# Routed experts on one core: weights in rows of 16 KB, tokens gathered by slot, two experts combined at once

## The chip, the core and the metric

The kernel runs on one core of a Trainium2 chip. A core has TensorE (PE, with its weight loads shown apart as PEld), VectorE (DVE), ScalarE (ACT), GpSimd (POOL) and SyncE (SP, which here only issues transfers), and 16 DMA engines that bring data from the chip's memory (HBM) into the on-chip memory of 128 partitions. The metric is the time of one launch in microseconds (us) on the device. The profiler records one launch with every instruction and every DMA packet; its span is the time from the first instruction to the last.

## The reference, cut to what matters

The program is two blocks of a model on 256 tokens of 1024 features in float32. The first block has two attentions, then the part that this change is about, then a gated embedding; the second block is a gated convolution and pooling, twice. The part in question sends every token to 4 of 32 experts:

```python
def routed_experts(h, w_router, b_router, w_gate_up, b_gate_up, w_down, b_down):
    logits = (hf @ w_router).astype(jnp.float32) + b_router.astype(jnp.float32)
    top_vals, top_idx = lax.top_k(logits, TOP_K)
    top_w = jax.nn.softmax(top_vals, axis=-1)
...
    def expert_block(args):
        xb, e = args
        gu = xb @ w_gate_up[e] + b_gate_up[e]
        g, u = gu[:, :D_EXPERT], gu[:, D_EXPERT:]
        g = jnp.minimum(g, SWIGLU_LIMIT)
        u = jnp.clip(u, -SWIGLU_LIMIT, SWIGLU_LIMIT)
        glu = g * jax.nn.sigmoid(SWIGLU_ALPHA * g)
        return ((u + 1.0) * glu) @ w_down[e] + b_down[e]
...
    y = jax.ops.segment_sum(yr * row_w[:, None].astype(yr.dtype), row_tok, num_segments=n + 1)[:n]
```

The sum y is added to the residual X. The weights of one expert are w_gate_up[e], 1024 x 2048 floats (8.39 MB), and w_down[e], 1024 x 1024 floats (4.19 MB): 12.58 MB for an expert and 402.7 MB for the 32. Each byte is used once.

## The kernel before, in words

Everything up to the router runs first. It leaves X (the residual), XS (the normed tokens, without their gains), and for each expert and token a rank in RM (its place among the tokens of that expert) and a weight in W. Then all 32 experts are computed one after the other by `static_expert`, each with 64 slots for tokens; what an expert has beyond 64 tokens is left to `further_block`, which runs in a loop behind a branch and isn't entered with these inputs.

For one expert, `load` issues on SP's queue 8 transfers of gate_up and 4 of down, each of 1 MB into a tile of 2048 columns. Row k * 128 + p of gate_up lies in partition p of tile k, so a partition gets one row of 8 KB; of down a tile holds two such rows of 4 KB. The tiles come from the pool `ring2`, 17 of them. A transfer is issued as soon as its tile is free and its turn on SP's queue has come. The products of the weights are 96 matmuls of 512 columns (64 for gate and up, 32 for down), each two instructions in the profile; they are those from `raw` to `bank`.

Around them, for each expert: `gather` makes a matrix of ones and zeros, OH, from the ranks (L777) and multiplies XS by it in 16 matmuls, of which XG, the tokens of the expert with features on partitions, comes out (L779 to L782, recorded at L150 as those of OH and XS); OW (L784) is the same with the weights in it, turned in two transposes (L810) and copied (L812). The activations of gate and up are on DVE and ACT (L803 to L807); their result is transposed (L823), copied (L825) and multiplied by down; the product is copied to yr (L832). `combine` then multiplies yr by the turned OW, 4 matmuls with the weights on 64 partitions, and adds each to X (L838 to L840).

Two things aren't in the order in which they are written. `combine` of expert e and `gather` for e + 1 are put behind the last product of gate and up (`gu_end`, with `issue_after`), so that they lie between those products and the ones of down. A scheduler of the language orders the rest by what is ready. The matmul helper `mm` is line L150, the transfers of `load` L176, those of `load_split` L193 with its scaled copies L198, and `row_rstd` has its squares at L284.

Behind the last expert, `ring2` is closed, and a new pool p3 takes the same memory: eight tiles for the rows of w_ple_gate are loaded into it, scaled on ACT (L198, `se`, `Yh` and `hi`), and their low halves made on POOL (L985, L987) or DVE (L989). Then the branch to the further blocks follows; behind it X is transposed (L946) and squared (L284), and the rest of the program runs.

Of the kernel before, what the change touches and what calls it, by code (L numbers as in the profile page):

```python
# [22 lines left out]
SL = 64  # L23
# [6 lines left out]
# columns of the constants that depend on shapes alone  # L30
# [12 lines left out]
# rows that every partition gets  # L43
# [52 lines left out]
def block_kernel(ctx: ExitStack, tc: tile.TileContext, a, out, dbg=None, ne=NE):  # L96
# [19 lines left out]
    def pair(at=None):  # L116
        """Room for the halves of 1024 columns."""
# [34 lines left out]
    def mm3(o, l, r, start, stop):  # L152
        """float32 product of operands split in halves of 12 bits each."""
# [4 lines left out]
    def split(raw, dst, eng=None):  # L158
        """raw = dst[0] + dst[1], both exact in the tensor engine's short float32."""
# [7 lines left out]
    def load(src, cn, size=2048, at=None):  # L167
        """Rows of src over (k, partition), a tile at a time, in turn in the tiles at where they are given."""
# [42 lines left out]
    tiles = {"adr": [ada_slot() for _ in range(3)]}  # L211
    hh, hl = [slot(s, dt=FR).rearrange("p (k n) -> p k n", k=KD) for s in ("s0", "s1")]
# [4 lines left out]
    wu, vv = slot("s2", 2560), slot("s5")  # L217
# [146 lines left out]
    # the rotated part of the keys that the heads share  # L364
# [6 lines left out]
    def rope(dst, src, T, half_, eng=None):  # L371
        """dst = src * cos + swapped src * sin, for heads [128, heads, 2 * half_] with the table of a token tile."""
# [7 lines left out]
    def head_root(src, hd, extra=None):  # L380
        """(mean of squares + eps) ** -0.5 of the heads [128, heads, d] over hd features."""
# [9 lines left out]
    roots_a, marks = [], []  # what fills gaps is issued behind the marks  # L391
# [32 lines left out]
    # the norm along the tokens, on every partition  # L424
# [61 lines left out]
    def values(hp, prs, Vt, dst):  # L486
        """The values of two heads, feature-major, in halves."""
# [104 lines left out]
    def branch_weights(n):  # L592
        """A tile for each 256 columns."""
# [5 lines left out]
    # sigmoid(z) = (tanh(z / 2) + 1) / 2; the half follows the output projection  # L599
# [23 lines left out]
    # the biases of gate and up: row p has expert p % 32's, low halves where p // 32 is odd,  # L623
    # the columns h * 512 to h * 512 + 511 of both for h = p // 64
# [31 lines left out]
    def logits(XT, h, pl):  # L656
        """The transposed half of X[:, t] times the router's weights; the norm's factor follows."""
# [72 lines left out]
    def further_list():  # L730
        """The further blocks of 64 rows of the experts that got more than 64."""
# [16 lines left out]
        # a row of the list for each partition that has one: its place, then its expert and first rank  # L748
# [471 lines left out]
```

## Time and profile before

| what | value |
|---|---|
| three runs | 1451.78, 1452.36, 1454.26 us; median 1452.36 |
| the profiled execution | span 1451.8 us, as long as the fastest run |
| PE busy | 1385.2 us (95%) |
| DVE, ACT, POOL busy | 594.2, 319.3, 320.9 us |
| bytes moved | 502.56 MB, mean 346 GB/s |
| time from the first expert's L803 to the last one's | 248.99 to 1172.49 us |
| granted TensorE clock, mean | 0.983 |

The page of a profile gives busy times over the whole span, then the span in 40 slices of 36.3 us. Slices 6 to 31 are the experts. A busy share there says that an engine had instructions running, not that it set the pace: PE and the DMA engines are both near full in these slices, and which of them the other waits for is seen only in the waits and in the timeline.

### The profile page before, as it was taken

The page shows a single profiled execution, that of the slowest core. Times are in us where ns is not written, and L with a number is a line of the kernel's source. Part 1 is how long each engine was busy: PE and PEld are TensorE (multiplying, and loading weights), DVE is VectorE, ACT ScalarE, POOL GpSimd, SP SyncE. Part 2 cuts the span into 40 slices and gives each one's busy share as a digit, 9 for nine tenths or more (in the row PEclk, how much of TensorE's full clock was granted, in tenths as well). Part 3 has the DMA queues.
Part 4 walks back from the last instruction along what each step waited for, and adds up shares of the span by engine and source line. Part 5 has one row for each costly group of instructions (what it writes and reads, how often), then busy time and mean ns, then how long its engine had stood idle before and what let it go on. Part 6 is the DMA issues. An engine that isn't in the chain of part 4 may idle for free. (4 is left out here: it accounts for less than half of the span.)

```text
span 1451.8 us, 18980 instructions
## 1 busy us (share of the span) xinstructions
PE 1385.2 (95%) x7599; PEld 795.1 (55%) x7599; DVE 594.2 (41%) x973; ACT 319.3 (22%) x598; POOL 320.9 (22%) x353
## 2 busy tenths in 40 slices
PE   7989999999999999999999999999999998889987
PEld 6788886344444444444443344444444347887986
DVE  4898954121322132213222222221321138688685
ACT  6745531000000000000000000000001135435432
POOL 5595461000000000000000000000000035785682
PEclk9989998999999999999999999999999999999999
DMA  9738789999999999999999999999999955756651
GB/s 332 239 119 305 263 305 401 417 417 418 417 415 416 418 418 416 415 417 418 418 416 416 417 417 418 417 415 417 417 418 415 417 226 189 232 176 202 202 190 44
DMA packets 144586, 502.56 MB, mean 346 GB/s; under 512 B 10288, under 2 KB 63792, under 8 KB 111472
## 3 DMA queue, kind: packets, MB, share of 16 engines
q1 hardware_dynamic: 143936, 500.60, 88.0%
q8 instruction: 61, 1.00, 0.3%
q10 hardware_dynamic: 560, 0.72, 0.2%
q14 instruction: 29, 0.24, 0.0%
HBM read 500.24 MB, written 1.05 MB: 345 GB/s over the span
## 5 line engine op out<-in xcount | busy, mean ns | idle before, releaser
L150 PE MATMUL bank<-raw,mid 128*64 128x512 f32 x3072 | 680.3, 598 | 1.9 <-ACT mid L825 1.4
L150 PEld LDWEIGHTS bank<-raw,mid 128*64 128x64 f32 x3072 | 215.1, 138 | 414.9 <-issue 387.9
L803 DVE TENSOR_SCALAR mid<-bank 128x512 f32<-128x512 f32 x32 | 22.1, 691 | 443.7 <-PE bank L150 443.7
L855 POOL CAST BIAS<-BIAS 128x128 fp32r<-128x128 f32 x32 | 10.2, 321 | 852.5 <-PE bank L150 852.4
L165 DVE TENSOR_TENSOR lo<-raw,hi 128x1024 fp32r<-128x1024 f32 (+2 forms) x91 | 116.1, 1296 | 21.3 <-ACT hi L160 20.9
L150 PE MATMUL bulk<-OH,XS 128*128 128x64 f32 x1024 | 121.6, 278 | 1.6 <-DVE OH L777 1.6
L150 PEld LDWEIGHTS bulk<-OH,XS 128*128 128x128 f32 x1024 | 120.2, 196 | 2.6 <-DVE OH L777 1.8
L160 ACT CAST hi<-raw 128x1024 fp32r<-128x1024 f32 (+1 forms) x102 | 105.8, 1041 | 68.0 <-PE bulk L150 57.5
L805 ACT ACTIVATE mid<-mid 128x512 f32<-128x512 f32 x32 | 20.1, 629 | 390.6 <-DVE mid L803 390.6
L150 PE MATMUL bulk<-mid,small 64*128 64x512 f32 x256 | 99.2, 628 | 7.1 <-DVE X L840 6.4
L784 DVE TENSOR_SCALAR OW<-cst,RM,SW 128x128 f32<-128x128 f32 x64 | 19.3, 344 | 172.1 <-PE bank L810 172.1
L840 DVE TENSOR_TENSOR X<-X,bulk 128x512 f32<-128x512 f32 x128 | 81.7, 679 | 9.0 <-PE bulk L150 9.0
L165 POOL TENSOR_TENSOR lo<-raw,hi 128x512 fp32r<-128x512 f32 x50 | 72.9, 1484 | 40.1 <-ACT hi L160 35.3
L812 ACT COPY small<-bank 128x256 f32<-128x256 f32 x32 | 11.9, 372 | 290.2 <-PE bank L810 290.2
L150 PEld LDWEIGHTS bulk<-mid,small 64*128 64x128 f32 x256 | 31.0, 185 | 74.8 <-issue 40.4
L150 PE MATMUL bulk<-hi,s 128*128 128x256 f32 (+2 forms) x256 | 59.3, 323 | 7.9 <-ACT hi L160 7.4
L150 PE MATMUL bulk<-s,hi 128*128 128x256 f32 x320 | 63.7, 296 | 0.0
L782 DVE TENSOR_TENSOR mid<-bulk,VC 128x512 f32<-128x512 f32 x32 | 22.1, 691 | 90.9 <-PE bulk L150 90.9
L556 DVE SCALAR_TENSOR_TENSOR acc<-adr,cact,acc 128x512 f32<-128x512 f32 x49 | 55.5, 1133 | 0.8 <-DMA adr<-in_w_ada_dram 0.3
L150 PEld LDWEIGHTS bulk<-s,hi 128*128 128x128 f32 x320 | 51.8, 197 | 1.0 <-DVE s L609 0.4
L559 POOL TENSOR_TENSOR adr<-adr,cact 128x512 f32<-128x512 f32 x32 | 44.5, 1412 | 34.3 <-DMA adr<-in_w_ada_dram 34.3
L150 PEld LDWEIGHTS bulk<-hi,s 128*128 128x128 f32 x256 | 43.9, 195 | 11.6 <-ACT hi L160 7.4
(442 smaller groups left out, 1906.0 us busy)
## 6 DMA issues: line engine op xcount, KB each, us to landing
raw<-in_w_gate_up_dram SPq DMA_DIRECT2D x256, 1024.0 KB, 19.8
raw<-in_w_down_dram SPq DMA_DIRECT2D x128, 1024.0 KB, 20.0
raw<-in_w_in_dram SPq DMA_DIRECT2D x75, 512.0 KB, 5.1
adr<-in_w_ada_dram SPq DMA_DIRECT2D x48, 512.0 KB, 4.5
raw<-in_w_out_dram SPq DMA_DIRECT2D x23, 512.0 KB, 3.8
raw<-in_w_ple_gate_dram SPq DMA_DIRECT2D x5, 512.0 KB, 15.8
raw<-in_w_branch_b_dram SPq DMA_DIRECT2D x4, 512.0 KB, 7.3
raw<-in_w_branch_a_dram SPq DMA_DIRECT2D x4, 512.0 KB, 5.4
```

What stands on the lines that cost most here:

```text
L150: nc.tensor.matmul(o, l, r, start=start, stop=stop)
L160: nc.scalar.copy(dst[0], raw)
L165: (eng or nc.vector).tensor_sub(dst[1][..., cs], raw[..., cs], dst[0][..., cs].bitcast(F32))
L556: e.scalar_tensor_tensor(v, w[:, k], cact[:, i + k:i + k + 1], v, op0=OP.mult, op1=OP.add)
L559: e.tensor_mul(w[:, k:k + 2], w[:, k:k + 2], cact[:, i + k:i + k + 2].unsqueeze(2).to_broadcast([P, 2, n]))
L782: nc.vector.tensor_mul(XG, pX.rearrange("p (k n) -> p k n", k=KD), bcol("g_ffn", 0, KD, SL))
L784: nc.vector.tensor_scalar(OW[:, t], io64d, rank(t), wgt(t), op0=OP.is_equal, op1=OP.mult)
L803: nc.vector.tensor_scalar(g_, pG, 7.0, None, op0=OP.min)
L805: nc.scalar.activation(sg, g_, AF.Sigmoid, scale=1.702)
L812: nc.scalar.copy(OT, pT[:, :S])
L840: nc.vector.tensor_add(xv, xv, pc)
L855: nc.gpsimd.tensor_copy(bs, ONE[:, e, :, None].bitcast(F32).to_broadcast([P, 2, SL]))
```

## The change

There are three parts. **Loads**: a new function, `load_rows`, puts r rows that follow one another in memory into one partition: 2 rows of gate_up (2 x 8 KB) or 4 rows of down (4 x 4 KB), so 16 KB without a gap. A tile has 4096 columns (2 MB), an expert 6 of them, and ring2 has 8 tiles, with OW and a new tile Y beside them. The order of the features in the products follows (XG's columns, `u[:, c::4]`, and new gains `g_rows`). **Gather**: OH becomes the operand that is held and XS the one that streams, so 4 matmuls of 512 columns give the tokens with slots on partitions; ACT copies them (XT), 4 transposes turn them, and DVE multiplies by the gains. **Combine**: OW of two experts lies in one tile, turned by 4 transposes for every second expert (`turn`), and split into a matrix of ones (OT) and the weights by slot (ws); the product of down is scaled by ws and kept in Y as a high half (ACT) and a low half (DVE) in the short float32 type; two experts are added to X by 8 matmuls over all 128 partitions.

```diff
-            return phase["ring2"].tile([P, 2048], F32, name="raw2", tag="raw2")
+            return phase["ring2"].tile([P, 4096], F32, name="raw2", tag="raw2")
...
+    def load_rows(src, cn, r, at=None):
+        blocks = src.rearrange("(b p r) n -> b p r n", p=P, r=r)
+        nb, parts = src.shape[0] // (P * r), {}
+        pr = r if at is None else 2048 // cn
+        def piece(b, i):
+            if (b, i) not in parts:
+                raw = (raw_slot() if at is None else at[len(parts) % len(at)])[:, :pr * cn]
+                raw = raw.rearrange("p (r n) -> p r n", r=pr)
+                nc.sync.dma_start(raw, blocks[b, :, i * pr:(i + 1) * pr])
...
-    def gather(rank, wgt):
+    def gather(rank, wgt, q, ow):
...
-            for k in range(KD):
-                mm(pX[:, k * SL:(k + 1) * SL], XS[:, t, k * P:(k + 1) * P], OH[:, t], t == 0 and k == 0,
-                   t == NT - 1 and k == KD - 1)
-        XG = mid([P, KD, SL])
-        nc.vector.tensor_mul(XG, pX.rearrange("p (k n) -> p k n", k=KD), bcol("g_ffn", 0, KD, SL))
...
+        for t in range(NT):
+            for g in range(2):
+                mm(pX[g * SL:(g + 1) * SL], OH[:, t], XS[:, t, g * 512:(g + 1) * 512], t == 0, t == NT - 1)
+        XT = mid([P, 512])
+        nc.scalar.copy(XT, pX)
+        pt = bulk()
+        for c in range(4):
+            nc.tensor.transpose(pt[:, c * P:(c + 1) * P], XT[:, (c // 2) * 256 + c % 2:(c // 2 + 1) * 256:2], ident)
+        XG = mid([P, 4, 2, SL])
+        nc.vector.tensor_mul(XG.rearrange("p c g n -> p (c g) n"), pt.rearrange("p (k n) -> p k n", k=KD),
+                             bcol("g_rows", 0, KD, SL))
...
+    def turn(ow):
+        pT = bank()
+        for i in range(2):
+            for t in range(NT):
+                nc.tensor.transpose(pT[:, (i * NT + t) * P:(i * NT + t + 1) * P],
+                                    ow[:, t, 2 * i:2 * i + 2].rearrange("p c n -> p (c n)"), ident)
+        OT, ws = mid([P, 2, S], FR), tiny([P, 2], "ws")
+        p3_ = pT.rearrange("p (i n) -> p i n", i=2)
+        nc.vector.tensor_scalar(OT, p3_, 0.0, None, op0=OP.is_gt)
+        nc.vector.reduce_sum(ws, p3_, axis=AX)
...
-        gu = load(gu_src, 2 * DE, at=at)
-        dn = load(dn_src, D) if at is None else None
+        gu = load_rows(gu_src, 2 * DE, 2, at)
+        dn = load_rows(dn_src, D, 4) if at is None else None
...
-        yr = mid([P, 512])
-        nc.scalar.copy(yr, py)
...
+        for g in range(2):
+            h, sl = g ^ q, slice(g * SL, (g + 1) * SL)
+            nc.scalar.activation(Y[sl, 0, h], py[sl], AF.Copy, scale=ws[sl, h:h + 1])
+            nc.vector.scalar_tensor_tensor(Y[sl, 1, h], py[sl], ws[sl, h:h + 1], Y[sl, 0, h].bitcast(F32),
+                                           op0=OP.mult, op1=OP.subtract)
...
+                for i in range(2):
+                    mm(pc, OT[sl, h, t * P:(t + 1) * P], Y[sl, i, h], i == 0, i == 1)
...
-    ready = gather(*rank_of(0))
-    ring2 = tc.tile_pool(name="ring2", bufs=17, reuse_waits="tile")
+    ring2 = tc.tile_pool(name="ring2", bufs=8, reuse_waits="tile")
+    pair_["ow"] = ow_tile()
+    ready = gather(*rank_of(0), 0, pair_["ow"])
```

The line numbers grow by 22 to 78: `mm` is L152 after the change, the transfers of `load_rows` are L197, `load_split` is L215 with its copies at L220, `turn` has L828, the transposes of XT L814, those of the activations L867, the high half of Y L878 and `row_rstd` L306.

On PE, the first place is around the end of the products of gate and up of one expert in the middle of the loop (`raw_...` are the tiles of weights, `mid` the yr, XG and activations, `small` the turned OW). Before, between the last gate_up tile and the first product of down there are combine, the transposes of the activations and the gather; the turned OW comes behind the biases:

```order
L150 MATMUL bank<-raw_4068,mid 64x512 x4
L150 MATMUL bulk<-mid,small 128x512 x4
L823 MATMUL bank<-cst,mid 128x128 x4
L150 MATMUL bulk<-OH,XS 128x64 x16
L150 MATMUL bank<-raw_4070,mid 64x512 x4
L150 MATMUL bank<-raw_4072,mid 64x512 x4
```

After the change two kinds of boundary take turns, here one without and one with a combine (both in the order in which PE has them):

```order
L152 MATMUL bank<-raw_3986,mid 64x512 x8
L152 MATMUL bulk<-XS,OH 64x512 x4
L867 MATMUL bank<-cst,mid 128x128 x4
L814 MATMUL bulk<-cst,mid 128x128 x4
L152 MATMUL bank<-raw_3988,mid 64x512 x8
...
L152 MATMUL bank<-raw_4092,mid 64x512 x8
L152 MATMUL bulk<-Y,mid 128x512 x6
L828 MATMUL bank<-cst,OW 128x128 x4
L152 MATMUL bulk<-Y,mid 128x512 x2
L152 MATMUL bulk<-XS,OH 64x512 x4
L867 MATMUL bank<-cst,mid 128x128 x4
```

The gather has 4 matmuls in place of 16 and 4 transposes more behind it; the combine has 8 for two experts in place of 4 for each; the turned OW has moved from behind the biases to the boundary.

On SP, the second place is the start of the experts' loads, with the semaphores for which each transfer waits (DMAHW is an earlier transfer). Before:

```order
L176 DMA raw_2696<-in_w_gate_up_dram 128x2048 [waits DMAHW6_49,DMAHW5_49,DMAHW1_49]
L176 DMA raw_2698<-in_w_gate_up_dram 128x2048 [waits DMAHW2_49]
L176 DMA raw_2700<-in_w_gate_up_dram 128x2048 [waits DMAHW3_49]
L176 DMA raw_2702<-in_w_gate_up_dram 128x2048 [waits DMAHW4_49,DVE_49]
L176 DMA raw_2704<-in_w_gate_up_dram 128x2048 [waits DMAHW5_49]
L176 DMA raw_2706<-in_w_gate_up_dram 128x2048 [waits DMAHW6_49,PE_49]
```

After:

```order
L197 DMA raw_2692<-in_w_gate_up_dram 128x4096 [waits DMAHW1_49]
L197 DMA raw_2694<-in_w_gate_up_dram 128x4096 [waits DMAHW2_49,DVE_49]
L197 DMA raw_2696<-in_w_gate_up_dram 128x4096 [waits DMAHW3_49,PE_49,DMAHW7_49,Activation_49,Pool_49]
L197 DMA raw_2698<-in_w_gate_up_dram 128x4096 [waits DMAHW0_49,PE_49,DMAHW4_49,Activation_49,Pool_49]
L197 DMA raw_2700<-in_w_down_dram 128x4096 [waits DMAHW5_49,PE_49,Pool_49]
```

Before, 3 MB wait for transfers alone; after, the first 2 MB do, and the second tile waits for DVE.

On ACT, the third place is the end of the experts, from behind the branch to the further blocks. Before, the copies into `se` and `Yh` stand ahead of the branch, and from behind it there are:

```order
L284 ACTIVATE mid,ss<-X 128x1024
L198 ACTIVATE hi<-raw,VC 128x1024
L950 CAST sa<-bank 128x4x128 x3
L198 ACTIVATE hi<-raw,VC 128x1024
L950 CAST sa<-bank 128x4x128
```

After:

```order
L306 ACTIVATE mid,ss<-X 128x1024
L1028 CAST sa<-bank 128x4x128 x2
L306 ACTIVATE mid,ss<-X 128x1024
L1028 CAST sa<-bank 128x4x128
L220 ACTIVATE se<-raw,VC 128x1024
L1028 CAST sa<-bank 128x4x128
L220 ACTIVATE Yh<-raw,VC 128x1024
L220 ACTIVATE hi<-raw,VC 128x1024 x3
```

All eight scaled copies of w_ple_gate now stand behind the branch, and the first of them behind both squares of X.

## Rows read from the trace of the kernel before

**Rows 1.** Page: engines over the span, then one DMA queue (packets, MB).

```profile
PE 1385.2 (95%) x7599; PEld 795.1 (55%) x7599; DVE 594.2 (41%) x973; ACT 319.3 (22%) x598; POOL 320.9 (22%) x353
...
q8 instruction: 61, 1.00, 0.3%
```

**Rows 2.** Windows in the experts: engines' busy us, PEclk, DMA share, GB/s.

```profile
300.00:500.00 200.00, 198.55 (x992) 84.82 (x990) 46.79 (x91) 15.21 (x28) 2.06 (x7) 1.00 1.02 417
503.00:518.00 15.00, 14.79 (x80) 7.36 (x78) 5.86 (x11) 1.21 (x2) 0.00 (x0) 1.00 1.02 423
553.00:558.00 5.00, 5.00 (x26) 1.62 (x24) 0.13 (x1) 0.58 (x1) 0.00 (x0) 1.00 1.03 410
```

**Rows 3.** DMA view of 503 to 518 us, then of 553 to 558 us.

```profile
DMA packets 870, 6.34 MB, mean 423 GB/s; under 512 B 96, under 2 KB 96, under 8 KB 96
...
DMA packets 532, 2.05 MB, mean 410 GB/s; under 512 B 31, under 2 KB 31, under 8 KB 532
```

**Rows 4.** Timeline of ACT, one instruction per expert: start us, us.

```profile
480.67 0.63 ACT L805 ACTIVATE mid<-mid 128x512 f32<-128x512 f32 x1 [13.02 <-DVE mid L803]
...
509.80 0.63 ACT L805 ACTIVATE mid<-mid 128x512 f32<-128x512 f32 x1 [13.02 <-DVE mid L803]
```

**Rows 5.** Timeline of PE over one expert's boundary.

```profile
509.75 1.98 PE L150 MATMUL bulk<-mid,small 64*128 64x512 f32 x6
511.94 1.12 PE L150 MATMUL bulk<-mid,small 64*128 64x512 f32 x2 [0.21 <-DVE X L840]
512.99 0.66 PE L823 MATMUL bank<-cst,mid 128*128 128x128 f32 x4
513.49 3.68 PE L150 MATMUL bulk<-OH,XS 128*128 128x64 f32 x32
517.10 5.37 PE L150 MATMUL bank<-raw,mid 128*64 128x512 f32 x24
```

**Rows 6.** Waits from 300 to 1100 us: us in total, times, longest.

```profile
PEld bank L150 <- DMA raw<-in_w_gate_up_dram: 10.7, 40, 0.3
PEld bank L150 <- DMA raw<-in_w_down_dram: 8.6, 27, 0.7
```

**Rows 7.** Timeline of DVE and PE: first and last expert.

```profile
248.99 0.69 DVE L803 TENSOR_SCALAR mid<-bank 128x512 f32<-128x512 f32 x1 [13.89 <-PE bank L150]
...
1172.49 0.69 DVE L803 TENSOR_SCALAR mid<-bank 128x512 f32<-128x512 f32 x1 [20.25 <-PE bank L150]
...
1177.80 7.09 PE L150 MATMUL bank<-raw,mid 128*64 128x512 f32 x32 [0.68 <-ACT mid L825]
...
1186.74 2.59 DVE L840 TENSOR_TENSOR X<-X,bulk 128x512 f32<-128x512 f32 x4 [8.98 <-PE bulk L150]
```

**Rows 8.** Start of the stage: timeline of SP and PE, then two windows.

```profile
186.74 19.06 SPq L176 DMA_DIRECT2D raw<-in_w_gate_up_dram  x8
...
234.32 15.48 PE L150 MATMUL bank<-raw,mid 128*64 128x512 f32 x64 [0.57 <-DVE mid L782]
...
199.00:203.30 4.30, 4.30 (x20) 3.34 (x19) 3.21 (x6) 2.48 (x5) 4.30 (x5) 1.00 0.05 21
203.30:218.00 14.70, 14.70 (x69) 12.20 (x68) 2.23 (x4) 2.83 (x4) 8.05 (x8) 1.00 0.99 401
```

**Rows 9.** Timeline behind the last expert: ACT, POOL and SP.

```profile
1185.42 1.15 ACT L198 ACTIVATE se<-raw,VC 128x1024 fp32r<-128x1024 f32 x1
...
1189.61 1.06 ACT L284 ACTIVATE mid<-X 128x1024 bf16<-128x1024 f32 x1 [2.00 <-DVEq L922]
...
1186.67 5.68 POOL L985 TENSOR_SCALAR raw<-raw,VC 128x1024 f32<-128x1024 f32 x2 [95.28 <-ACT se L198]
...
1193.15 7.53 SPq L193 DMA_DIRECT2D raw<-in_w_in_dram  x5
```

**Rows 10.** Windows where the granted clock falls.

```profile
787.00:790.40 3.40, 2.44 (x7) 0.84 (x6) 1.66 (x3) 0.41 (x1) 0.00 (x0) 1.00 1.01 420
790.40:797.20 6.80, 6.80 (x14) 2.02 (x14) 1.37 (x2) 0.00 (x0) 0.29 (x1) 0.50 1.01 411
```

More of the change, by code (lines that the diff above doesn't have):

```diff
@@ L770, in down_biases, with places @@
                 nc.vector.tensor_add(xv, xv, pb)
-    def gather(rank, wgt):
-        OH, OW = [work.tile([P, NT, n], F32, name=s, tag=s, bufs=2) for s, n in (("OH", SL), ("OW", P))]
+    def places(ow, t, q):
+        return ow[:, t, 0::3] if q == 0 else ow[:, t, 1:3]
+    def gather(rank, wgt, q, ow):
+        OH = work.tile([P, NT, SL], F32, name="OH", tag="OH", bufs=2)
         pX = bulk()
@@ L807, in expert @@
         nc.vector.tensor_mul(u, u, sg)
-        pT = bank()
-        for t in range(NT):
-            nc.tensor.transpose(pT[:, t * P:(t + 1) * P], OW[:, t], ident)
-        OT = small([P, S])
-        nc.scalar.copy(OT, pT[:, :S])
-        nxt = None
         with tc.issue_after(gu_end):
@@ L817, in expert @@
                 late.pop()()
-            if after_gu:
-                nxt = after_gu()
-        dn = dn or load(dn_src, D, at=at)
+            OT, ws = between()
+        dn = dn or load_rows(dn_src, D, 4, at)
         ph = bank()
         for c in range(4):
-            nc.tensor.transpose(ph[:, c * P:(c + 1) * P], u[:, c * P:(c + 1) * P], ident)
+            nc.tensor.transpose(ph[:, c * P:(c + 1) * P], u[:, c::4], ident)
         hT = mid([P, 4, P])
@@ new lines, in expert, with combine, ow_tile @@
+        return OT, ws
+    def combine(OT, Y, alone=False):
+        for t in range(NT):
+            for h in range(2):
+                pc, sl = bulk(), slice(h * SL, (h + 1) * SL) if alone else slice(0, P)
+                for i in range(2):
+                    mm(pc, OT[sl, h, t * P:(t + 1) * P], Y[sl, i, h], i == 0, i == 1)
+                xv = X[:, t, h * 512:(h + 1) * 512]
+                nc.vector.tensor_add(xv, xv, pc)
+    def ow_tile():
+        return phase["ring2"].tile([P, NT, 4, SL], F32, name="OW", tag="OW", bufs=2)
@@ L848, in rank_of, with y_tile, static_expert, between @@
+    def y_tile():
+        return phase["ring2"].tile([P, 2, 2, 512], FR, name="Y", tag="Y", bufs=1)
     def rank_of(e):
         return lambda t: RM[:, t, e:e + 1], lambda t: W[:, t, e:e + 1]
-    def static_expert(e, ready):
-        def after():
-            return gather(*rank_of(e + 1))
+    pair_ = {}
+    def static_expert(e, XG):
+        q, nxt = e % 2, []
+        def between():
+            if e + 1 < ne:
+                if q:
+                    pair_["next"] = ow_tile()
+                nxt.append(gather(*rank_of(e + 1), 1 - q, pair_["next" if q else "ow"]))
+            return (pair_["OT"], pair_["ws"]) if q else turn(pair_["ow"])
+        if q == 0:
+            pair_["Y"] = y_tile()
@@ L854, in static_expert @@
         bs = sel[e % 2]
         nc.gpsimd.tensor_copy(bs, ONE[:, e, :, None].bitcast(F32).to_broadcast([P, 2, SL]))
-        return expert(*rank_of(e), bs.rearrange("p h n -> p (h n)"),
-                      a["w_gate_up"][0, e], a["w_down"][0, e], after if e + 1 < ne else None, ready)
+        pair_["OT"], pair_["ws"] = expert(XG, q, bs.rearrange("p h n -> p (h n)"), a["w_gate_up"][0, e],
+                                          a["w_down"][0, e], pair_["Y"], between)
+        if q:
+            OT, Y = pair_["OT"], pair_["Y"]
+            if e + 1 < ne:
+                late.append(lambda: combine(OT, Y))
+                pair_["ow"] = pair_["next"]
+            else:
+                combine(OT, Y)
```

59 lines of the change are left out of this document (33 added, 26 removed).

## The prediction

> **What bounds the kernel now.** I read the page first, then windows over the experts, then the timelines of one expert on ACT and PE, then the waits.
>
> The page shows PE busy for 95% of the span [rows 1]; that alone doesn't say that PE sets the pace. In the window from 300 to 500 us PE is busy for 198.55 of 200 us, and in the same time the DMA share is 1.02 and 417 GB/s flow [rows 2]. Both are full. The same instruction of two experts stands 509.80 - 480.67 = 29.13 us apart [rows 4]: this is PE's period, since over 800 us PE waits only 10.7 + 8.6 us for weights [rows 6]. An expert has 12.583 MB; at 417 GB/s that is 30.2 us, more than 29.13. That PE doesn't wait can only come from a lead: the ring is full when PE begins, and the transfers lose it slowly. From the first expert's L803 to the last one's there are 1172.49 - 248.99 = 923.5 us for 31 periods [rows 7], 29.79 each; 31 x 29.13 is 903.0, so some 20.5 us are extra work put between experts (the biases of down, the list of further blocks, the product of w_ple_proj). So PE ends the stage, with DMA just behind. Either one alone can be made faster for little: what counts is what the change does to both.
>
> **The rate of the loads.** A stretch with rows of 8 KB alone moves 423 GB/s, one with rows of 4 KB alone 410 [rows 2]. The packets there are of those sizes: in the second, all 532 are under 8 KB, in the first 96 of 870 [rows 3]. With 16 engines, 8192 x 16 / 423 = 309.9 ns for a packet of 8 KB, and 4096 x 16 / 410 = 159.8 ns for one of 4 KB. The difference, 150.1 ns, is what 4 KB cost; 9.7 ns are left as a fixed part. By this line 16 KB take 4 x 150.1 + 9.7 = 610.1 ns, or 429.7 GB/s. Two thirds of the bytes at 423 and one third at 410 would be 418.6, the long window has 417, so I take 429.7 x 417 / 418.6 = 428. An expert then takes 29.4 us instead of 30.2, and 32 save 25 us. Bounds: if nothing above 8 KB helps, 423 (421.4 with the same factor); if the fixed part vanished, 4096 x 16 / 150.1 = 436.6 (435).
>
> The Trainium skill, "DMA: Bandwidth & Descriptors", section "Why small descriptors are slow (HBM only)", gives some 3 cycles for each packet, which at the page's 850 MHz is an estimated 3.5 ns, a third of the 9.7 ns above. An expert gives each of 16 engines 64 packets of gate_up and 64 of down before, 48 in all after; by the page the 80 packets less would save 0.28 us per expert and 9 us in all, by the trace's 9.7 ns 0.78 and 25. With 3.5 ns the stretch of 4 KB rows would move 418 GB/s beside the 423; it moves 410, so the trace decides.
>
> **PE's work.** From 509.75 to 517.10 us PE does nothing of the weights: combine, the transposes of the activations, the gather [rows 5], 7.35 us; 21.78 us are left, of which 0.4 are the turned OW that moves into the boundary. Prices: 24 instructions of 512 columns take 5.37 us, 0.22 each [rows 5]; four transposes 0.5 to 0.66. The gather becomes 8 instructions (1.8 us, before 3.68) and 4 transposes behind an ACT copy of 512 columns that the trace has at L825 with 0.59; the transposes of the activations lie in between, so I count 0.6 for the transposes and 0.6 for what is not hidden. A boundary without combine: 1.8 + 0.5 + 0.6 + 0.6, about 3.6. One with it has 8 one-pass instructions (1.8), 4 transposes of OW (0.6) and some waiting for DVE, whose queue has X's additions and OW ahead of the activations' last step: about 6.4. The mean is 5.0, the period 21.4 + 5.0 = 26.4. If nothing were gained it is 29.13 as now; if each boundary were 3.6, 25.0. The scaling of Y is on ACT and DVE, busy 15.21 and 46.79 of 200 us [rows 2], behind the last product of down, and its reader comes an expert later: nothing.
>
> So after the change PE needs 26.4 and DMA 29.4 us: DMA sets the pace, and PE's gain is worth only the lead that it no longer has to catch up.
>
> **Start of the stage.** SP issues the first loads at 186.74; DMA nearly stands still from 199.00 to 203.30 (21 GB/s: the free tiles are loaded, the next waits), then moves 401 GB/s up to 218 [rows 8], 5.9 MB. Before, the 3 MB that wait for transfers alone were in by 199; after, it is one tile of 2 MB, as the second waits for DVE. The later waits are for the same releases, in coarser tiles: 8.0 MB by 218 instead of 9.0, a loss of 2.5 us. The ninth tile waits until PE is through with the first, PE's first weights are at 234.32 and take 15.48 us for 64 instructions [rows 8], so 3.9 for a tile of 2 MB; the ring of 16.8 MB is full at 218 + 8.8 MB / 428 = 238.6, PE frees the tile about then or shortly behind: a gap of 2.5 us (0 to 4).
>
> **The end.** Loads in the stage: 402.7 MB and 1.3 MB for the embedding. 404.0 - 8.0 = 396.0 MB at 428 take 925.2 us: 218 + 925.2 + 2.5 = 1145.7, and 1147 if the rate is 427.4. From 1147, half of down's products follow: 3.5 us, by 7.09 for 32 instructions [rows 7]; 1.3 for Y; the combine and its additions 3.75, by 1185.58, where combine starts behind the copy of the last product, to the end of X's additions at 1186.74 + 2.59 = 1189.33 [rows 7]. 1147 + 3.5 + 1.3 + 3.75 = 1155.6: X is done 33.7 us sooner.
>
> Behind it I add 5 us. Before, the copies into `se` and `Yh` run at 1185.42 and ahead of the end of X, so that POOL starts on the low halves at 1186.67; X's squares come at 1189.61, and SP's loads of w_in at 1193.15 [rows 9]. After, `se`'s copy stands behind the branch and behind two squares of 1.06 us on ACT, so POOL's 5.68 us start some 6 us later against X, and what POOL holds (the next weights' halves, the tiles for SP's loads) follows. If the program behind has slack, 0; if all of it passes on, 8. Another 3 us are for the slips of a PE that now waits for each tile. **Sum**: 1451.8 - 33.7 + 5 + 3 = 1426.1, so 1426 us. The profiled execution, 1451.8, is 0.6 below the median of 1452.36, less than counts here: I take 0.2% (2.9 us) as what can be told from no change.
>
> **The rivals.**
> A, the forecast: chance 0.66. With the fixed part gone (435 GB/s) 396.0 MB take 910.3 us, 15 less: 1411. With the costs at the end at 8 instead of 5: 1429.
> B, rows of 16 KB move no faster than today's mix, since the share already reads 1.02 [rows 2] and the chip or memory could be what is full: 396.0 / 417 = 949.6 us, 24 more than A: 1450. For it: the 423 and 410 are single stretches. Against: they differ by more than the mix explains. Chance 0.12, of which 0.09 is no change and 0.03 just faster.
> C, a gain up to 8 KB alone, since the transfers could be cut there: 396.0 / 421.4 = 939.7 us, 14.5 more: 1440. Chance 0.08.
> D, slower: PE's clock. At one place inside the experts PE was busy for 2.44 of 3.40 us up to 790.40, and in the 6.80 us behind the granted clock is 0.50, 1.2 of 2.4 GHz [rows 10]; this costs 3.4 us. Now every boundary has waits (ACT copy, DVE's queue) and every tile may bring one. If each expert paid it, PE's period is 26.4 + 3.4 = 29.8, and X is done 31 x (29.8 - 29.13) = 21 us later than before, with the 8 behind it 1481. PE becomes the bound above a period of 29.13 - 33.7 / 31 = 28.04, and the kernel slower than now above 29.13 - 8 / 31 = 28.87, so 2.5 us lost per expert decide. Against: at the boundary shown, where PE stands still for 0.21 us, no clock falls, and a clock that falls from waiting for DMA uses up the time that PE would wait anyhow. Chance 0.11.
> The Trainium skill, "TensorE: Matmul & The Clock Gate", section "HAM oscillation — how this bites in real kernels", has this rule: where the work on a tile is shorter than the wait for the next, the clock is throttled at each tile. It speaks against this change, which lets PE wait; rows 10 agree that a wait can do it, and D is its price.
> E, packets of 16 KB are slow: the only ones in the trace (61 of 1.00 MB on another queue) take 0.3% of 16 engines' span, 1.14 us each [rows 1], which would be 230 GB/s and over 2200 us. They share the engines with a full queue, so I give it 0.03.
>
> **How the numbers follow.** The likeliest is A, 1426. From 1411 to 1452 the range holds A, C and B, 0.86 by the chances, and leaves out D and E. Faster by over 0.2%: A, C and a part of B, 0.77; the same 0.09; slower D and E, 0.14.
>
> **What would show it.** Right: GB/s of 426 to 430 throughout the experts; packets of 16 KB; waits of PE for gate_up and down of 2 to 3 us per expert in place of 19.3 us in 800; the period at 29.3 to 29.5, X's end near 1156. If 417 stays, B; 421, C. Wrong in PE's part: a boundary over 7 us, or PEclk at 0.50 in every expert (D). Wrong at the end: if the time from X's end to the end of the span, now 1451.8 - 1189.33 = 262.5 us, grows by less than 2 or more than 10.

## The result, and the profile after

The change takes 1433.86 us in the median (1431.79 to 1438.36), the kernel before 1452.66 us beside it: a ratio of 0.9876, with an interval of 0.9865 to 0.9888, so 18 to 19 us or 1.2% faster. The prediction of 1426 us was right in sign and cause and held the time in its range, and it counted on 8 us more gain than came. The profiled execution has a span of 1433.8 us, 18.0 under that of before. A span isn't the time of the launch: the profiled one took 1435.64 us, about 2 more, so the span of 1451.8 us before is not "as long as the fastest run", and the prediction's sum, which starts from it, is a span as well: 1426.1 beside 1433.8.

The page of the changed kernel, beside [rows 1]:

```profile
PE 1306.5 (91%) x6831; PEld 706.2 (49%) x6831; DVE 626.0 (44%) x1005; ACT 351.6 (25%) x630; POOL 321.0 (22%) x353
...
DMA packets 100546, 502.44 MB, mean 350 GB/s; under 512 B 7216, under 2 KB 60720, under 8 KB 75632
```

PE has 79 us less to do, and the time fell by 18: most of what PE won is now waiting. The windows show where the pace comes from, beside [rows 2]:

```profile
300.00:500.00 200.00, 190.68 (x880) 69.71 (x878) 58.87 (x110) 23.98 (x38) 2.08 (x7) 1.00 1.01 428
300.00:1100.00 800.00, 740.84 (x3332) 265.25 (x3329) 214.88 (x401) 89.31 (x141) 8.00 (x27) 0.99 1.01 428
```

428 GB/s, to the figure of the prediction, over 800 us. The waits in the same 800 us, beside the 10.7 and 8.6 us of [rows 6]:

```profile
PEld bank L152 <- DMA raw<-in_w_gate_up_dram: 72.4, 42, 3.5
...
PE bank L152 <- DMA raw<-in_w_gate_up_dram: 37.6, 34, 2.7
```

The first row is PE's weight loads, the second its matmuls: both now wait for weights, the loads 2.7 us per expert (2 to 3 forecast), all for gate_up. The timeline of ACT (L856 stands where L805 stood), beside [rows 4], first where the ring is still full, then where it has been emptied:

```profile
301.34 0.63 ACT L856 ACTIVATE mid<-mid 128x512 f32<-128x512 f32 x1 [11.48 <-DVE mid L854]
...
329.08 0.63 ACT L856 ACTIVATE mid<-mid 128x512 f32<-128x512 f32 x1 [11.44 <-DVE mid L854]
...
354.51 0.63 ACT L856 ACTIVATE mid<-mid 128x512 f32<-128x512 f32 x1 [11.48 <-DVE mid L854]
...
523.99 0.63 ACT L856 ACTIVATE mid<-mid 128x512 f32<-128x512 f32 x1 [15.72 <-DVE mid L854]
...
553.35 0.63 ACT L856 ACTIVATE mid<-mid 128x512 f32<-128x512 f32 x1 [13.07 <-DVE mid L854]
```

Early, PE sets its own period: 27.74 and 25.43 us by turns, 26.6 in the mean (26.4 forecast). Where the ring is empty the distance is 29.36 us at both kinds of boundary, in each of the six periods from 524 to 700 us: that is the transfers' (29.4 forecast). Behind the extra work of some experts PE is late and catches up for some periods at 25.4 to 27.7 us before it waits again. The boundary with a combine, on PE, beside [rows 5]:

```profile
520.36 3.65 PE L152 MATMUL bank<-raw,mid 128*64 128x512 f32 x16 [1.25 <-DMA raw<-in_w_gate_up_dram]
523.94 1.66 PE L152 MATMUL bulk<-Y,mid 128*128 128x512 f32 x6
525.44 0.60 PE L828 MATMUL bank<-cst,OW 128*128 128x128 f32 x4
525.79 0.71 PE L152 MATMUL bulk<-Y,mid 128*128 128x512 f32 x2
526.72 1.94 PE L152 MATMUL bulk<-XS,OH 128*64 128x512 f32 x8 [0.21 <-DVE X L891]
528.69 0.74 PE L867 MATMUL bank<-cst,mid 128*128 128x128 f32 x4
529.35 0.75 PE L814 MATMUL bulk<-cst,mid 128*128 128x128 f32 x4
530.11 3.65 PE L152 MATMUL bank<-raw,mid 128*64 128x512 f32 x16
```

6.2 us from 523.94 to 530.11, where 6.4 were counted, and PE waits 1.25 us for a tile ahead of it. The end, on DVE, PE and ACT, beside [rows 7] and [rows 9]:

```profile
1146.46 0.69 DVE L854 TENSOR_SCALAR mid<-bank 128x512 f32<-128x512 f32 x1 [10.67 <-PE bank L152]
...
1165.48 1.97 DVE L891 TENSOR_TENSOR X<-X,bulk 128x512 f32<-128x512 f32 x3 [0.16 <-PE bulk L152]
...
1149.59 0.75 PE L867 MATMUL bank<-cst,mid 128*128 128x128 f32 x4 [2.32 <-DVE mid L858]
1151.01 10.08 PE L152 MATMUL bank<-raw,mid 128*64 128x512 f32 x32 [0.68 <-ACT mid L869]
1163.37 3.35 PE L152 MATMUL bulk<-Y,mid 128*128 128x512 f32 x8 [2.28 <-ACT Y L878]
...
1175.16 1.65 PE L152 MATMUL bulk<-hi,sa 128*128 128x512 f32 x3 [5.44 <-ACT hi L220]
...
1171.39 1.17 ACT L220 ACTIVATE se<-raw,VC 128x1024 fp32r<-128x1024 f32 x1
```

X is done at 1165.48 + 1.97 = 1167.45 us, 21.9 sooner than before; the prediction had 1155.6. From the first L854 (249.70 us) to the last it is 896.8 us, 26.7 less than before; from the last L854 to X's end 21.0 us instead of 16.8, and from there to the end of the span 266.4 instead of 262.5. So -26.7 is given back by 4.2 and 3.9, and the first L854 comes 0.7 later.

### The profile page after: what moved, and what is told of

It reads as the page before. It is cut to its first block, busy times and chain, and to the rows that moved or that the text cites. A ratio compares the mean times of both kernels' runs of the same rounds, so it can differ in the third digit from the quotient of the medians.

```text
span 1433.8 us, 17081 instructions
## 1 busy us (share of the span) xinstructions
PE 1306.5 (91%) x6831; PEld 706.2 (49%) x6831; DVE 626.0 (44%) x1005; ACT 351.6 (25%) x630; POOL 321.0 (22%) x353
## 5 line engine op out<-in xcount | busy, mean ns | idle before, releaser
L152 PE MATMUL bank<-raw,mid 128*64 128x512 f32 x3072 | 692.5, 603 | 43.7 <-DMA raw<-in_w_gate_up_dram 37.6
L152 PEld LDWEIGHTS bank<-raw,mid 128*64 128x64 f32 x3072 | 213.5, 138 | 484.2 <-issue 399.0
L854 DVE TENSOR_SCALAR mid<-bank 128x512 f32<-128x512 f32 x32 | 22.1, 692 | 392.8 <-PE bank L152 392.8
L879 DVE SCALAR_TENSOR_TENSOR Y<-bank,ws,Y 64x512 fp32r<-64x512 f32 x64 | 48.0, 750 | 250.3 <-ACT Y L878 250.3
L856 ACT ACTIVATE mid<-mid 128x512 f32<-128x512 f32 x32 | 20.2, 631 | 436.3 <-DVE mid L854 436.3
L878 ACT ACTIVATE Y<-bank,ws 64x512 fp32r<-64x512 f32 x64 | 43.7, 682 | 280.2 <-PE bank L152 254.1
L152 PE MATMUL bulk<-XS,OH 128*64 128x512 f32 x256 | 63.2, 614 | 4.7 <-DVE X L891 3.2
L152 PE MATMUL bulk<-hi,s 128*128 128x256 f32 (+2 forms) x256 | 59.7, 325 | 8.0 <-ACT hi L162 7.5
L152 PE MATMUL bulk<-s,hi 128*128 128x256 f32 x320 | 62.8, 293 | 0.0
L152 PEld LDWEIGHTS bulk<-s,hi 128*128 128x128 f32 x320 | 51.1, 195 | 0.7 <-DVE s L608 0.2
L152 PEld LDWEIGHTS bulk<-hi,s 128*128 128x128 f32 x256 | 44.2, 196 | 11.7 <-ACT hi L162 7.5
L152 PE MATMUL bulk<-sc,hi 128*128 128x256 f32 x144 | 42.9, 298 | 3.9 <-DVE se L1219 2.1
L152 PE MATMUL bulk<-sa,hi 128*128 128x256 f32 x144 | 42.9, 298 | 3.8 <-DVE sb L1219 2.1
L152 PE MATMUL bulk<-s,lo 128*128 128x256 f32 x160 | 45.9, 291 | 0.0
L891 DVE TENSOR_TENSOR X<-X,bulk 128x512 f32<-128x512 f32 x64 | 42.3, 682 | 1.1 <-PE bulk L152 0.7
L152 PE MATMUL bulk<-lo,s 128*128 128x256 f32 (+2 forms) x128 | 41.7, 327 | 0.9 <-DVE lo L167 0.9
```

Of the source, the lines that this page charges most:

```text
L152: nc.tensor.matmul(o, l, r, start=start, stop=stop)
L854: nc.vector.tensor_scalar(g_, pG, 7.0, None, op0=OP.min)
L856: nc.scalar.activation(sg, g_, AF.Sigmoid, scale=1.702)
L878: nc.scalar.activation(Y[sl, 0, h], py[sl], AF.Copy, scale=ws[sl, h:h + 1])
L879: nc.vector.scalar_tensor_tensor(Y[sl, 1, h], py[sl], ws[sl, h:h + 1], Y[sl, 0, h].bitcast(F32), op0=OP.mult, op1=OP.subtract)
L891: nc.vector.tensor_add(xv, xv, pc)
```

## The experiments

**1. The rows alone.** The kernel of before with `load_rows`, tiles of 2 MB and a ring of 8:

```diff
-        gu = load(gu_src, 2 * DE, at=at)
+        gu = load_rows(gu_src, 2 * DE, 2, at)
...
-                mm(pX[:, k * SL:(k + 1) * SL], XS[:, t, k * P:(k + 1) * P], OH[:, t], t == 0 and k == 0,
+                mm(pX[:, k * SL:(k + 1) * SL], XS[:, t, (k // 2) * 256 + k % 2:(k // 2 + 1) * 256:2], OH[:, t], t == 0 and k == 0,
...
-    ring2 = tc.tile_pool(name="ring2", bufs=17, reuse_waits="tile")
+    ring2 = tc.tile_pool(name="ring2", bufs=8, reuse_waits="tile")
```

> The loads of the change (rows of 16 KB, 6 tiles of 2 MB, a ring of 8) with the gather and combine of before. My theory: PE sets the end of the stage before the change, so faster loads alone give nothing: the period of one expert stays at 29.1 us, PE does not wait, the DMA engines are held back by full tiles and move about 12.58 MB / 29.79 us = 422 GB/s on average, and the time is 1446 to 1454 us, within 6 us of before. Rival: the rows are the whole gain and the new gather and combine are idle decoration; then the time is that of the change, 1434 us.

Measured: 1463.75 us, ratio 1.0076 (1.0059 to 1.0093). No gain, as the theory said, but a loss of some 10 us that it had not (1446 to 1454 us expected). Two things besides the rows had moved. The first tile of the ring lay on memory that comes free late, so that SP issued the first load at 219.37 us and not at 186; and the gather now read XS with a stride of two (32 instructions in 3.88 us, not 3.68). The run is not a clean half of the change; run 5 repeats it without the two.

**2. The work alone.** The change with the same tiles, but rows that lie apart:

```diff
-        blocks = src.rearrange("(b p r) n -> b p r n", p=P, r=r)
+        blocks = src.rearrange("(b r p) n -> b p r n", p=P, r=r)
...
-            nc.tensor.transpose(ph[:, c * P:(c + 1) * P], u[:, c::4], ident)
+            nc.tensor.transpose(ph[:, c * P:(c + 1) * P], u[:, c * P:(c + 1) * P], ident)
```

> The gather and combine of the change and its tiles of 2 MB in a ring of 8, but with rows apart: a tile of gate_up is filled by two rows of 8 KB per partition that lie far apart in memory, one of down by four rows of 4 KB. My theory: the rate hangs on the length of a contiguous row, so 417 GB/s return, the transfers set the end, and 396 MB take 949.6 us instead of 925.2, 24 us more than with the change, less some 3 us by which PE then keeps up better: 1453 to 1459 us, no better than before. Rival one: the rate comes from 2 MB per transfer and fewer transfers; then 428 GB/s and 1434 us. Rival two: PE's shorter work is what gained; then 1434 to 1440 us.

Measured: 1456.45 us, ratio 1.0028 (1.0017 to 1.0040). A window and two instructions of that run's ACT timeline, of experts that follow one another:

```profile
300.00:1100.00 800.00, 721.97 (x3257) 251.99 (x3255) 209.87 (x394) 85.50 (x135) 7.92 (x27) 0.99 1.02 417
```

```profile
500.24 0.63 ACT L856 ACTIVATE mid<-mid 128x512 f32<-128x512 f32 x1 [15.33 <-DVE mid L854]
...
530.36 0.63 ACT L856 ACTIVATE mid<-mid 128x512 f32<-128x512 f32 x1 [16.27 <-DVE mid L854]
```

417 GB/s and a period of 30.12 us. Transfers are as few and as large as in the change, so it is the length of the row, not that of the transfer, that gives 428; both rivals fall. Between 30.12 and 29.36 us there are 0.76 us for 80 packets less on each engine, 9.5 ns per packet: the 9.7 ns of the prediction. It isn't the estimated 3.5 ns that the prediction worked out from the Trainium skill ("DMA: Bandwidth & Descriptors", section "Why small descriptors are slow (HBM only)"). The run also shows that PE's shorter work alone, in the coarser ring, gains nothing: with it the kernel is even 0.3% slower than before, and why isn't shown.

**3. A filler behind the last expert.** Five matmuls that nobody reads, behind the last products of gate and up:

```diff
+            if e + 1 == ne:
+                po = spare()
+                for _ in range(5):
+                    mm(po, ident, XS[:, 0, :512], True, True)
```

> The change, with 5 matmuls of 512 columns added behind the last expert's products of gate and up, in the 2.3 us in which PE waits for the activations; nothing reads their result. My theory: in the change PE's clock falls to 0.5 behind that gap and half of the last down products run at it, so that 10.1 us are spent on 32 instructions where 7.1 would do; with the gap filled the clock stays at 1.0, and the end comes 2 to 3 us sooner: 1431 us. Rival: the second half of the last down tile lands at about 1153 us, and PE waits for it, so that the clock costs nothing or under 1 us.

Measured: 1433.71 us, ratio 0.9869 (0.9853 to 0.9886), the same as the change. The timeline of PE there:

```profile
1148.20 4.56 PE L152 MATMUL spare<-XS,cst 128*128 128x512 f32 x10
1152.59 0.63 PE L867 MATMUL bank<-cst,mid 128*128 128x128 f32 x4
1153.90 7.09 PE L152 MATMUL bank<-raw,mid 128*64 128x512 f32 x32 [0.68 <-ACT mid L869]
```

The clock did what was expected (7.09 us in place of 10.08), but the filler of 4.56 us was longer than the gap of 2.3, and the products began 2.9 us later. The time doesn't tell the theory from its rival. The 32 products do: they take 7.09 us in one go, here and in runs 6 and 8, so PE doesn't wait for the last tile.

**4. Tiles and copies behind the experts in another order.** `sd`, `sc`, `sb` and `Yl`, which are needed late, take the memory of Y, OW and the ring's first tile; the value that the branch needs is read behind all eight loads on SP and the third copy on ACT:

```diff
-    room = [slot("se", dt=FR), slot("Yh", dt=FR)]
-    further = [slot("sd")]
+    further = [slot("sd"), slot("sc", N_PUW)]
+    ow_far = slot("sb")[:, :NT * 4 * SL].rearrange("p (t c n) -> p t c n", t=NT, c=4)
+    Y_far = slot("Yl", dt=FR).rearrange("p (i h n) -> p i h n", i=2, h=2)
...
+    room = [slot("se", dt=FR), slot("Yh", dt=FR)]
...
-    n = nc.values_load(LSI[0:1, NLIST:NLIST + 1], min_val=0, max_val=NLIST)
+    with tc.issue_after(copies[2]), tc.issue_after(loads[-1]):
+        n = nc.values_load(LSI[0:1, NLIST:NLIST + 1], min_val=0, max_val=NLIST)
```

> The change, with the tiles behind the experts laid out in another order (the ones that are needed late lie on Y, OW and the ring's last tile), all eight loads of w_ple_gate put ahead of the branch on SP, and the first three scaled copies ahead of it on ACT. My theory: of the time from the end of X's additions to the end of the program, 266.4 us with the change and 262.5 before, the 3.9 us come from these copies, and PE's wait of 5.4 us for them goes: 258 to 262 us behind X, 1427 to 1430 us in all. Rival: POOL or SP sets the pace behind the experts whatever ACT does, and the time stays at 1434; or the loads of w_ple_gate take bandwidth from the last expert, and X's end comes up to 5 us later.

Measured: 1428.87 us, ratio 0.9842 (0.9825 to 0.9860), faster than the change, and the time in the expected span. ACT and then PE in that run's timeline:

```profile
1160.74 1.15 ACT L220 ACTIVATE se<-raw,VC 128x1024 fp32r<-128x1024 f32 x1
...
1164.45 1.94 PE L1027 MATMUL bank<-cst,X 128*128 128x128 f32 x16 [1.21 <-DVEq L1003]
1166.21 0.50 PE L152 MATMUL bulk<-hi,sa 128*128 128x512 f32 x1
```

`se` is made ahead of the branch, and PE goes from the transposes of X to the first product without the 5.44 us of waiting. From X's end (1164.2) to the end of the span it is 262.1 us (258 to 262 expected), as before the change. So the 3.9 us behind X are the cost of the copies' place. The loads of w_ple_gate start at 1155.10 us and not at 1161.13, when the last products of down have ended. Where the tiles lie and what is issued ahead of the branch were changed together, and no run separates them. X's end, 3.2 us sooner than in the change, is no part of this: PE's work up to there is the same, but its 32 products of down took 8.46 us in this launch, 10.08 in that.

**5. The rows alone, without the side effects.** Run 1 with the ring's tiles placed as in the change and XS written in the order of the rows:

```diff
+    phase["ring2"].tile([P, 2560], F32, name="pad", tag="pad", bufs=1)
...
-        nc.vector.tensor_scalar(XS[:, t], X[:, t], r, None, op0=OP.mult)
+        nc.vector.tensor_scalar(XS[:, t].rearrange("q (b j p) -> q b j p", b=4, j=2),
+                                X[:, t].rearrange("q (b p j) -> q b j p", b=4, j=2), r, None, op0=OP.mult)
```

> The loads of the change with the gather and combine of before, as the first of these runs, with its two side effects taken out: the tiles of the ring lie where the change has them, so that the first loads start at about 187 us and not at 219, and XS is written in the order of the new rows, so that the gather reads it without a stride (3.88 us for 32 instructions there, 3.68 before). My theory: PE sets the end with these loads, at 29.1 to 29.2 us per expert with about 20 us of extra work in three experts, X ends at 1189 to 1192 us, and the time is 1450 to 1456 us, no better than before; DMA waits for free tiles. Rival: the loads alone bring the gain, 1434 to 1440 us.

Measured: 1461.24 us, ratio 1.0070 (1.0049 to 1.0092); the profiled execution, with a span of 1456.7, is the shortest of it. Its ACT timeline and the window:

```profile
509.99 0.63 ACT L828 ACTIVATE mid<-mid 128x512 f32<-128x512 f32 x1 [13.45 <-DVE mid L826]
...
539.21 0.63 ACT L828 ACTIVATE mid<-mid 128x512 f32<-128x512 f32 x1 [13.45 <-DVE mid L826]
```

```profile
300.00:1100.00 800.00, 791.23 (x3887) 336.78 (x3885) 185.15 (x366) 58.57 (x108) 7.92 (x27) 0.99 1.00 422
```

29.22 us: PE's period, 0.09 us more than before. DMA could move 428 and moves 422, PE is busy for 791 of 800 us, and no wait for weights is among that stretch's waits. X ends at 1193.7 us, 4.4 later than before. The theory's mechanism stands, and the rival is out, but the time is above the 1450 to 1456 us expected. The median is 9.6 us above that of the kernel before, run beside it (1451.61), while X ends only 4.4 us later, and it is 2.4 us above the time of the profiled execution (1458.86); both stay open.

**6. The fourth run with a short filler.** As run 4, and run 3's edit with `range(2)`.

> The order of tiles and copies behind the experts of the fourth run, and 2 matmuls of 512 columns (4 instructions, 1.8 us) in place of the 5 (4.6 us) behind the last expert's products of gate and up; nothing reads them. My theory: the filler of 4.6 us was 2.1 us longer than the gap of 2.3 us and so gave back what the clock had won; 1.8 us fit into it, the clock stays at 1.0, the 32 instructions of the last down take 7.1 us instead of 10.1 (8.5 in the fourth run), and X ends 1.4 to 3 us sooner than there: 1425.5 to 1427.5 us. Rival: the last tile's landing at 1153 us holds PE whatever its clock, and the time stays at 1429.

Measured: 1427.21 us, ratio 0.9824 (0.9806 to 0.9841), not told apart from run 4. On PE:

```profile
1148.84 0.74 PE L867 MATMUL bank<-cst,mid 128*128 128x128 f32 x4 [0.40 <-DVE mid L858]
1150.26 7.09 PE L152 MATMUL bank<-raw,mid 128*64 128x512 f32 x32 [0.68 <-ACT mid L869]
1159.63 3.59 PE L152 MATMUL bulk<-Y,mid 128*128 128x512 f32 x8 [2.28 <-ACT Y L878]
...
1156.00:1162.00 6.00, 3.72 (x14) 1.94 (x11) 2.21 (x4) 3.76 (x5) 1.15 (x1) 0.82 1.01 401
```

The products of down take 7.09 us as expected, and the combine behind the next gap of 2.28 us takes 3.59 instead of 2.48 in run 4. X ends at 1163.9 us, 0.3 sooner, where 1.4 to 3 were expected: that the time lies in its span is luck. So the filler took the loss out of down, and the loss behind the second gap stayed (0.82 from 1156 to 1162 us), which the change has too: there the granted clock is 0.50 from 1164 to 1166 us, in the combine of 3.35 us. In run 3, with the longer filler, it is 1.00 behind a second gap of 2.27 us, and the combine takes 2.48.

**7. The old gather.** The change with the 16 matmuls of 64 columns:

```diff
+            for k in range(KD):
+                mm(pX[:, k * SL:(k + 1) * SL], XS[:, t, k * P:(k + 1) * P], OH[:, t], t == 0 and k == 0,
+                   t == NT - 1 and k == KD - 1)
...
-        XT = mid([P, 512])
-        nc.scalar.copy(XT, pX)
```

> The change with the gather of before (16 matmuls of 64 columns, no copy and no transposes of XT; XS written in the order of the rows). My theory: PE's period in stretches in which it does not wait for weights was 25.43 and 27.74 us by turns, 26.6 in the mean, against 29.36 for the transfers; the old gather costs 0.6 to 1.1 us more, 27.2 to 27.7, still under the 28.0 at which PE would become the bound, so the time stays within 4 us of the change: 1433 to 1438 us. Rival: PE has no such slack, because the three experts with extra work eat it, and the time goes up by 10 us or more.

Measured: 1441.66 us, ratio 0.9925 (0.9907 to 0.9943): 8 us of the 18 are gone, and the theory falls. Three instructions of its ACT timeline, and its waits for weights from 300 to 1100 us:

```profile
529.55 0.63 ACT L852 ACTIVATE mid<-mid 128x512 f32<-128x512 f32 x1 [11.48 <-DVE mid L850]
558.86 0.63 ACT L852 ACTIVATE mid<-mid 128x512 f32<-128x512 f32 x1 [11.37 <-DVE mid L850]
585.46 0.63 ACT L852 ACTIVATE mid<-mid 128x512 f32<-128x512 f32 x1 [11.48 <-DVE mid L850]
...
PEld bank L152 <- DMA raw<-in_w_gate_up_dram: 15.5, 10, 2.1
```

29.3 and 26.6 us by turns, 27.95 in the mean: the old gather costs 1.37 us per expert, not 0.6 to 1.1. And it waits for weights for only 15.5 us in 800, the last time at 758 us: from there on PE, with the extra work of its experts, is the bound, and X ends at 1173.7 us, 6.2 later than with the change. The theory had a price too small by 0.3 to 0.8, and no account of how the extra work adds up. The threshold of 28.04, from the prediction, was somewhat too high: at 27.95 already 7.8 us are lost; 27.95 - 7.8 / 31 = 27.7 is an estimate of it.

**8. The last pair in plain float32.** As run 6, and for the last two experts:

```diff
+        if last:
+            nc.scalar.activation(Y[0:SL, 0, q].bitcast(F32), py[0:SL], AF.Copy, scale=ws[0:SL, q:q + 1])
+            nc.vector.tensor_scalar(Y[SL:P, 0, 1 - q].bitcast(F32), py[SL:P], ws[SL:P, 1 - q:2 - q], None, op0=OP.mult)
+            return OT, ws
```

> The sixth run, and for the last two experts Y is kept in plain float32: the two halves of the columns are scaled side by side, one on ACT and one on DVE, and the combine reads float32 (4 matmuls of two instructions each instead of 8 of one). My theory: from the last product of down to the start of the combine 2.3 to 3 us pass in ACT, DVE, ACT, DVE one behind the other; two copies side by side take 0.75, so X ends 1.5 to 2.2 us sooner than in the sixth run, and the time is 1423.5 to 1426 us, under both kernels. Rival: the end behind the experts waits for the loads of w_ple_gate and their halves on POOL, not for X, and the time stays at that of the sixth run.

Measured: 1428.02 us, ratio 0.9839 (0.9820 to 0.9857), no gain over runs 4 and 6. On PE, and a window:

```profile
1159.94 3.70 PE L152 MATMUL bulk<-Y,mid 128*128 128x512 f32 x8 [1.58 <-DVE Y L878]
...
1156.00:1162.00 6.00, 4.42 (x17) 1.63 (x14) 1.49 (x3) 3.16 (x4) 1.77 (x1) 1.00 0.98 369
```

DVE's half begins only behind ACT's, so that PE waits 1.58 us instead of 2.28, and the combine in float32 takes 3.70 us at a clock of 1.00: 0.46 for each of its 8 instructions, as for the 10 float32 instructions of run 3's filler (4.56 us), where the short type took 2.48 for 8 in runs 3 and 4. X ends at 1164.4 us. From the last L854 to X's end it is 17.6 us, 0.6 less than in run 6. The expected 1.5 to 2.2 us didn't come: the wait got only 0.7 us shorter, and the combine is no shorter than run 6's at its fallen clock. The rival's reason isn't needed for it.

## Why the prediction was right, and where its size was off

**The pace.** Right in each step that the rows show. The line through 4 KB and 8 KB, scaled to the mix, gave 428 GB/s, and 428 was measured; 29.4 us per expert and 29.36; PE at 26.4 and 26.6. Runs 2, 5 and 7 show that all parts are needed: rows alone leave PE at 29.22, work alone leaves the transfers at 30.12, and either is 0.3 to 0.7% slower than before; with rows and the new combine but the old gather PE is at 27.95, and 10 us are gained; with all, 18. "What counts is what the change does to both" is shown by these four. A slip of count: an expert has 48 matmuls in 96 instructions, not 96 matmuls; the sums used instructions.

**The end of the transfers.** The step "218 + 925.2 + 2.5", 1147 at its lower rate, is the first that was mis-sized: the last tile lands at 1153.1 us (issued at 1119.7, 33.4 us to landing). Windows around the ring's first turn and the end of the loads, in the change:

```profile
218.00:225.00 7.00, 6.21 (x44) 5.18 (x42) 4.99 (x18) 2.41 (x9) 3.72 (x8) 0.77 0.97 385
...
236.00:240.00 4.00, 4.00 (x14) 1.21 (x12) 0.00 (x0) 0.00 (x0) 0.00 (x0) 0.64 0.60 254
240.00:244.00 4.00, 4.00 (x22) 1.36 (x20) 0.00 (x0) 0.00 (x0) 0.00 (x0) 1.00 0.68 197
...
1145.00:1147.00 2.00, 2.00 (x12) 0.53 (x8) 0.54 (x1) 0.00 (x0) 0.00 (x0) 1.00 0.85 360
1147.00:1150.00 3.00, 0.68 (x5) 0.42 (x4) 2.23 (x4) 0.63 (x1) 0.00 (x0) 1.00 0.56 240
1150.00:1156.00 6.00, 5.32 (x15) 1.62 (x16) 0.00 (x0) 0.59 (x1) 0.00 (x0) 0.52 0.13 52
```

The gap at the ninth tile is there, at the place forecast, with (428 - 225.5) x 8 / 428 = 3.8 us instead of 2.5, and from 218 to 225 us 0.7 us are missing. The largest part had no term in the sum: from 1145 to 1147 us the rate falls to 360 GB/s (0.3 us), and behind 1147 the last 1.0 MB come at 240 and then 52 GB/s, in 6.1 us where 428 would need 2.4 (3.7 us). With the shares of 0.56 and 0.13 the 16 engines don't finish together; why they spread so far isn't shown. Together 6.0 of the 6.1 us.

**From the last tile to X's end.** 3.5 + 1.3 + 3.75 = 8.55 us were counted, 1167.45 - 1153.1 = 14.35 measured. Half of down's products were to follow the last tile at full clock. This step has the wrong path: PE doesn't wait for the last tile. Its last wait for a weight in the stage is for the last tile of gate_up, two tiles ahead (first row below); the products of gate and up end at 1147.26, and the activations follow, so that down starts at 1151.01:

```profile
1143.35 0.14 PEld L152 LDWEIGHTS bank<-raw,mid 128*64 128x64 f32 x2 [0.40 <-DMA raw<-in_w_gate_up_dram]
...
1133.31 13.95 PE L152 MATMUL bank<-raw,mid 128*64 128x512 f32 x64
```

At full clock down would end at 1151.01 + 7.09 = 1158.1, 1.5 us behind 1153.1 + 3.5. The clock wasn't full: in the last expert there is neither a gather nor a combine between gate and up and the transposes, PE stands for 2.32 us, and behind it the granted clock is 0.52 (last window above). Down takes 10.08 us, 3.0 more, and ends at 1161.1. Y waits 2.28 us, not 1.3, because ACT and DVE take turns on its four pieces, and the combine with X's additions is 4.1 us, not 3.75. Together X's end is 11.9 us late, of which the 3 us for slips had covered a part. Runs 3, 6 and 8 took the clock's loss from down (7.09 us). Run 6 kept the loss in the combine; runs 3 and 8 had none there, but the first had too long a filler and the second a dearer combine. The loss itself is that of single launches: with the same products, run 4 lost 1.4 us in down, the change 3.0.

**Behind X.** 5 us were counted, 3.9 measured, and run 4 shows the cause that was given, the place of the copies, by taking them back: it is at 0.9842 of before, and neither run 6 nor run 8, which add to it, is told apart from it.

**The rivals.** B and C are out by 428, E too. D is out as a price that each expert pays: PE mostly waits up to 1.5 us for a tile, and the granted clock is 1.00 from 500 to 560 us and 0.99 in the mean from 300 to 1100. But the clock does fall in three places from 300 to 1100 us, among them one behind a wait of 2.65 us for a tile:

```profile
500.00:560.00 60.00, 54.08 (x248) 18.96 (x246) 15.09 (x28) 6.33 (x10) 0.59 (x2) 1.00 1.01 427
...
727.28 5.19 PE L152 MATMUL bank<-raw,mid 128*64 128x512 f32 x16 [2.65 <-DMA raw<-in_w_gate_up_dram]
...
728.00:732.00 4.00, 4.00 (x16) 1.25 (x14) 0.34 (x1) 0.00 (x0) 0.00 (x0) 0.70 0.98 418
```

The 16 products take 5.19 us there instead of 3.65. The other two are in the extra work of experts, where PE waits for DVE several times over (0.52 from 778 to 782 us, 0.50 from 896 to 900). The rule that the prediction took from the Trainium skill ("TensorE: Matmul & The Clock Gate", section "HAM oscillation — how this bites in real kernels") is for work on a tile that is shorter than the wait for the next. Here the work is 3.65 us and the wait mostly up to 1.5, so the rule's condition isn't met, and it didn't speak against this change.

## What to carry to other kernels

Where two resources are both near full, read the period of each alone (bytes over the measured rate, and the distance of one instruction in a stretch without waits) before spending work on one: here each half of the change by itself lost a little, and together they won 1.2%. A fixed cost per packet can be read from two stretches of the same trace with packets of different size, and it carried over to a third size: 428 GB/s by the line, scaled to the mix, and 428 measured. At the end of a stage, follow the work that must come behind each of the last tiles, not behind the last one alone. When a pool takes over another's memory, look at what lies on the tile that is released last: 5 us hung on the order of the allocations and of the issues together.

## What the runs showed of the hardware that was not expected

The clock fell behind a gap of 2.32 us at the end of the experts and behind a wait of 2.65 us in the middle of them, and did not from 500 to 560 us, where PE waits as often as every 5 us for up to 1.5 us. A gap of 2.3 us isn't always followed by a fall: behind the one ahead of the combine the granted clock is 1.00 in runs 3 and 4, and it fell to 0.50 in the change and in run 6 (1164 to 1166 us, and 1160 to 1162). Neither filler gained time that the runs can tell. A gather with weights read at a stride of two costs 3.88 us for 32 instructions where contiguous ones take 3.68, and the four transposes of columns at a stride of four take 0.74 us, where contiguous ones take 0.66 (the change and run 2).
